# A macaron encoder block in split fp32: the norm's factor moved behind the SwiGLUs' last products, and the first bytes of its SBUF tiles moved

## The chip, the cores and the metric

The kernel runs on one core of a Trainium2 chip, in one launch. The metric is the device time of that launch in microseconds. The kernel before takes 2161.77 us, the median of three runs (2161.57 to 2161.9).

## What is computed

x is 1024 tokens by 1024 features in fp32; a SwiGLU has 2816 hidden features.

```python
def rmsnorm(x, g):
    return x * rsqrt(mean(x * x, -1) + eps) * g

def swiglu_ffn(x, w_in, w_out):
    gate, up = split(x @ w_in, 2)
    return (silu(gate) * up) @ w_out

h = x + 0.5 * swiglu_ffn(rmsnorm(x, norm_ffn1), ffn1_w_in, ffn1_w_out)
u = rmsnorm(h, norm_mix)
q, k, v, g_ret, p, gates = split(u @ w_in)
ret  = headwise_rmsnorm(retention(rotary(q), rotary(k) / 16, v)) * silu(g_ret)
pool = multiscale_pool(p)
gate = sigmoid(gates + gate_bias)
h = h + (gate[0] * (ret @ w_ret_up) + gate[1] * (pool @ w_pool_up)) @ w_out
h = h + 0.5 * swiglu_ffn(rmsnorm(h, norm_ffn2), ffn2_w_in, ffn2_w_out)
return rmsnorm(h, norm_final)
```

The factor of a norm, rsqrt(mean + eps), is one number for each token. It commutes with a matrix product, so the kernel multiplies un-normed features and applies the factor later. In `silu(gate) * up` the gate needs it before silu; the up half is only multiplied, so its factor may come at any later place, behind `w_out` too.

## The kernel before

**Products.** Activations lie with features on the 128 partitions and tokens along the free axis (two halves of 512). TensorE (PE) works on fp32 in two pieces: `split` (L153 to L155) makes a high part by a copy on ScalarE (ACT) and a low part by a subtraction on VectorE (DVE); `split_scaled` (L157 to L159) does so with a factor. `mm3` (L172 to L176) then makes each product from three matmuls, high x high (L174), high x low (L175), low x high (L176). The stationary operand is 128 x 128, "the weights" below; the moving operand is 128 x 512, or 128 x 256 at the second level.

**Strassen.** `strassen` (L421) forms a 2 x 2 block product from seven products on combinations of the weights' blocks (L11, S1 to S4, ...) and of the activations' blocks (R11, T1 to T4, ...), with results in PSUM banks `a`, `b` and `e`. Two of the seven, with R21 and with R22, are done for pairs of groups by another Strassen level (`common`, L527): three steps of 14 small products of three matmuls each. Their weights are the tiles `wx`, `ws12`, `ws34` and `wy`, and their moving operands are blocks `y1` to `y4` that `blocks` (L341) makes once for a norm, beside blocks of R21 and R22 themselves. This gives 43 blocks of 42 matmuls of 256 columns in the whole kernel: 15 in the first SwiGLU, 10 in the projections, 18 in the second SwiGLU.

**Order.** `Flow` (L57) runs over steps. Each step has a `prep` (loads, combinations and splits) and a `body` (matmuls and evacuation); a prep is issued LOOK = 4 steps ahead of its body. Everything else waits in one list of background work (`flow.add`), of which `rate` entries, one or two, are issued after each body. What stands under `soon()` gets a high priority. A scheduler orders each engine's instructions from this. All loads and stores go through SyncE's (SP's) queue.

**The SwiGLU's first half** (`ffn_in`, L699) has 22 groups, each one 128-row tile of gate and one of up. `evac` (L713) takes results out of PSUM. If the rows of the norm's factor (`nx.rb`, one 128 x 1024 tile with the factor of each token on all partitions) exist already, and the result is not to be added to another, the factor is multiplied in on the way (L718). Otherwise the plain value is written, and a multiplication by the factor goes into the background list (L722). Both are done for the gate and for the up half, by halves of 512 tokens. At a group's end (`end`, L724) come the silu (ACT, L728) and the product of gate and up in two halves (L731); for every second group the combinations of two hidden tiles that the next half needs are formed and stored to DRAM.

**The SwiGLU's second half** (`ffn_out`, L801) has the products p1, p6, p2, p7, p5, p3 and p4 (L819 on), each a loop over the 11 pairs of hidden tiles; p1 and p6 alternate, and so do p2 and p7. Eight tiles `acc` (128 features x 1024 tokens) are loaded with the residual at k = 6 of p1 (L829 to L832). `after1` to `after4` (L898 to L938) add each finished PSUM bank, times 0.5, to its quarters (`onto`, L891): P1 goes into a small tile `h` and from there into three quarters. Then `sink` takes a finished quarter on to the next norm (sums of squares). In the second SwiGLU the seventh product is turned round, with tokens on the partitions: `near` (L957) prepares the T4 blocks with a factor 0.5 and does two of four token tiles step by step, `far` the other two; `last.seed` and `last.finish` belong to the final norm (`Last`), which scales `dacc` and stores.

**Tiles.** All tiles come from pools whose buffers lie one behind another in SBUF. `weights` (L166) takes a tile of 1024 + LINE floats, LINE = 64, and lets the weights start `at` floats behind its beginning. `at` is 0 for first-level products. For the second level it is APART = 48 floats (192 bytes), except `wy` where the block `y4` lies in a buffer of the tag `t4`: those have 0 (`near`, L269 and L347, L547). `ss` tiles hold sums (8 floats). In the built program the first bytes within a partition are these:

| tile or tag | before | modulo 256 | after | modulo 256 |
|---|---|---|---|---|
| `ones_r` | 3040 | 224 | 3072 | 0 |
| `c2` (from) | 3552 | 224 | 3584 | 0 |
| `t4` (from) | 19936 | 224 | 19968 | 0 |
| `raw` (from) | 56800 | 224 | 56832 | 0 |
| `wt` (from; 4352 bytes each) | 73248 | 32 | 73472 | 0 |
| `mv` (from) | 95008 | 32 | 95232 | 0 |
| `tl` (from) | 209696 | 32 | 209920 | 0 |
| second-level weights inside `wt` | +192 | 224 | +88 | 88 |

The first byte of the weights less that of the moving operand, modulo 256, is as follows. First-level products have 0 before and after, since the tags `wt` and `mv` both lie at 32, later both at 0. Second-level products have 192 before where the block lies in `mv` or `tl`; where it lies in `t4`, `ws34` with `y3` has 0 and `wy` with `y4` has 64. After, all of them have 88. In the retention, the products with `kd` and those of the scores have 0, those with `sm` 192 and those of the state with `q` 64. After, all of these have 0.

Of the kernel before, what the change touches and what calls it, by code (L numbers as in the profile page):

```python
# [17 lines left out]
P = 128  # L18
S = 1024
# [71 lines left out]
def block_kernel(ctx: ExitStack, tc, x, x_tok, vecs, f1_in, f1_out, w_in, w_v, pool_w, w_ret, w_pool, w_o,  # L91
# [170 lines left out]
    class Next(Norm):  # L262


        def __init__(self, name, gain, keep=None):
            super().__init__(name)
            self.gain, self.keep = gain, keep
            self.M, self.Y, self.made, self.ready, self.tiles, self.t1s, self.rb = {}, {}, {}, set(), {}, {}, None
            self.near = set()  # L269

        def quarter(self, mt, tokens, tile):
            src = tile[:, tokens]
# [68 lines left out]
        def blocks(self, R, tags, over=False):  # L341

            left, x = dict(zip(("y3", "y2", "y4") if over else ("y1", "y3", "y2", "y4"), tags)), {}
            if left["y4"][0] == "t4":  # L347
                self.near.add(R)

            def sums(z):  # L350
                for i in range(2):
                    m = self.M[R, 2 * i + z]
                    v = c2(f"{self.name}x{i}{z}")
                    tt(v, m[:, 0].bitcast(F32), m[:, 1].bitcast(F32), ADD)
                    x.update({(i, j, z): half_of(v, j) for j in range(2)})

            def difference(n, z):

                x00, x01, x10, x11 = (x[i, j, z] for i in range(2) for j in range(2))
                to, p, q = {"y1": (x00, x01, x00), "y3": (x01, x11, x01), "y2": (x00, x11, x00),  # L360
                            "y4": (x00, x10, x00)}[n]
                tt(to, p, q, SUB)
                if n not in left:
                    m, at = self.M[R, z], HI
                else:
                    tag, bufs = left[n]
                    if (R, n) not in self.made:

                        self.made[R, n] = sb.tile([P, 2, H], F32R, tag=tag, bufs=bufs, name=f"{self.name}{R}{n}")
                    m, at = self.made[R, n], (LO, HI)[z]  # L370
                self.Y[R, n, z] = parts(m, at)
                split(m[:, 0, at], m[:, 1, at], to)
                if z and n == "y4":
                    self.ready.add(R)

            work = []
            for z in range(2):
                work.append(lambda z=z: (sums(z), difference("y1", z)))
                work.append(lambda z=z: difference("y3", z))
                work.append(lambda z=z: (difference("y2", z), difference("y4", z)))  # L380
            return work
# [145 lines left out]
    def common(nx, A, B, n):  # L527
# [171 lines left out]
    def ffn_in(nx, w, ops, name, start=None):  # L699
# [4 lines left out]
        def group(g):  # L704
            gate_up = {}

            def dest(which):
# [2 lines left out]
                    gate_up[tile] = (tl if start and g == 0 else t4)(f"{name}{'gu'[tile]}{g}")  # L710
                return half(gate_up[tile], j)

            def evac(which, in0, in1):  # L713
                j, dst = which[1], dest(which)
                if in1 is not None:
                    tt(dst, in0, in1, ADD)
                elif nx.rb is not None:
                    tt(dst, in0, half(nx.rb, j), MUL)  # L718
                    return
                else:  # L720
                    copy(dst, in0)
                flow.add(lambda: tt(dst, dst, half(nx.rms(), j), MUL))  # L722

            def end():  # L724
                gate, up = gate_up[0], gate_up[1]

                def swish():
                    act(gate, gate, AF.Silu)  # L728

                def times(j):  # L730
                    tt(half(up, j), half(gate, j), half(up, j), MUL)  # L731
# [66 lines left out]
    ops_done = {}  # L798


    def ffn_out(ops, ready, w, res, name, sink, end, last=None):  # L801

        R, T, B, T4 = ops
        t, acc = {}, {}
        S1, S2, S3 = {}, {}, {}

        def kept(store, n, k):
            if k % 2 == 0:  # L810
# [12 lines left out]
        def p1(k):  # L823
            flow.until(lambda: k in ready)
            r = tl(f"{name}r{k}")
            load(r, R[k])
            ra = raw(f"{name}ra{k}")
            load(ra, w[k, :, :S])
            if k == 6:  # L829
                for mt in range(KT):  # L830
                    acc[mt] = t4(f"{name}acc{mt}")
                    load(acc[mt], res[mt])  # L832
# [10 lines left out]
            return s2, half(t["r"], 1)  # L843

        def p2(k):
            r = tl(f"{name}q{k}")
# [8 lines left out]
        def p7(k):  # L855
            return half(S3[k // 2], k % 2), half(t["r"], 1)

        def p5(k):
            return half(S1[k // 2], k % 2), both("T1", k, lambda z: B[z][:, :H])

        def p3(k):
            return half(S2[k // 2], k % 2), both("R22", k, lambda z: T[z][:, H:])

        def p4(k):
            return both("L22", k, lambda z: w[z, :, 2 * H : 3 * H]), both("T4", k, lambda z: T4[z])

        bk = {}
# [20 lines left out]
        def quarter(mt, j):  # L888
            return half(acc[mt], j)

        def onto(mt, j, where, i, last=True):  # L891
            q = quarter(mt, j)
            with soon():
                stt(q, bk[where, i], 0.5, q, MUL, ADD)
            if last:
                flow.add(lambda: sink(mt, slice(j * H, (j + 1) * H), acc[mt]))

        def after1(i):  # L898
            h = c2(f"{name}p1{i}")
            with soon():  # L900
                act(h, bk["a", i], AF.Copy, scale=0.5)
                tt(quarter(i, 1), quarter(i, 1), h, ADD)

            def rest():
                for j in (1, 0):
                    tt(quarter(i + 4, j), quarter(i + 4, j), h, ADD)

            flow.add(rest)

        def after6(i):  # L910
            onto(i, 1, "b", i, False)

        def after2(i):
            onto(i, 0, "a", i)

        def after7(i):
            onto(i + 4, 1, "b", i, False)
            if last:

                onto(i + 4, 0, "b", i, False)  # L920
                if i == 3:
                    flow.add(*last.turned(acc))

        def after5(i):
            onto(i + 4, 1, "a", i)

        def after3(i):
            onto(i, 1, "a", i)
            if i == 3:
                end(0)  # L930

        def after4(i):
            onto(i + 4, 0, "b", i)
            if i == 3:
                end(1)

# [74 lines left out]
    x_sums = sb.tile([P, 8], F32, tag="ss", bufs=2, name="x_sums")  # L1011

    def x_square(t):
        r = tl(f"xs{t}")
# [15 lines left out]
    def ffn1():  # L1030
        for n, step in enumerate(ffn_in(first, f1_in, ops1, "a", lead)):
            flow.rate = 1 if n < 40 else 2
            yield step
        yield from ffn_out(ops1, ops_done["a"], f1_out, x, "b", mix.quarter, end1)

    mix = Next("n2", V_MIX, h1)

# [328 lines left out]
    class Unit:  # L1366
# [5 lines left out]
        def loads(self):  # L1372
# [9 lines left out]
            if self.nh == 0:  # L1382
                self.dec = sb.tile([P, H], F32, tag="dec", bufs=1, name=f"dec{self.h}")
                load(self.dec, decay[self.h])
                self.ss = sb.tile([P, 8], F32, tag="ss", bufs=2, name=f"ss{self.h}")
                self.O = {}

        def follow(self, u):
# [278 lines left out]
    class Last(Norm):  # L1667
# [15 lines left out]
        def turned(self, acc):  # L1683


            def gains():
                self.row = sb.tile([P, S], F32, tag="mv", bufs=N_MV, name=f"{self.name}row")
                load(self.row, g_row)
                self.ssq_e = sb.tile([P, 8], F32, tag="ss", bufs=2, name=f"{self.name}sse")

            def done(n):

# [72 lines left out]
    flow.run(chain(ffn1(), projections(), retention(), merge(), second(),  # L1765
                   ffn_out(ops2, ops_done.setdefault("c", set()), f2_out, h2, "d", fin.quarter, fin.end, fin)))
    flow.some(-1)


# [84 lines left out]
```

## Time and profile before

| | |
|---|---|
| median of three runs | 2161.77 us |
| the profiled execution | 2165.61 us |
| its span, first to last instruction | 2163.8 us |
| SwiGLU 1, first half | 0 to about 432 us |
| SwiGLU 1, second half | to about 667 us |
| projections | to about 1181 us |
| retention and pooling's products | to about 1370 us |
| merge and output projection | to about 1524 us |
| SwiGLU 2, first half | to about 1942 us |
| SwiGLU 2, second half and final norm | to 2164 us |

The stages are read from the names of the matmuls' outputs: a tile's name begins with the letter of its stage (`a` and `b` for the first SwiGLU's two halves, `c` and `d` for the second's), and digits are left out of the groups. The page gives the busy time of each engine with its share of the span, then slices, the chain of work that ended last, and groups of instructions. PE's matmuls are pipelined: one row of the timeline starts well before the one ahead of it has ended, so the time of a matmul is read from one start to the next and not from its own length. By the rows of stages, the retention keeps PE and DVE busy like this (columns: stretch, length, then for PE, weight load, DVE, ACT and POOL the busy time and count, the granted clock, the DMA engines' mean share and GB/s):

```profile
1181.00:1370.00 189.00, 188.19 (x1170) 167.93 (x1169) 150.77 (x300) 114.81 (x271) 0.00 (x0) 1.00 0.61 208
1942.00:2164.00 222.00, 215.11 (x967) 177.70 (x965) 165.85 (x292) 104.04 (x195) 0.00 (x0) 0.99 0.54 182
```

The second row is the last half of the second SwiGLU with the final norm, where PE is without work for 6.9 us, most of it behind the last matmul.

### The profile page before, as it was taken

What the parts mean: (1) busy time and instruction counts of PE and PEld (TensorE: products, weight loads), DVE (VectorE), ACT (ScalarE), POOL (GpSimd) and SP (SyncE); (2) the same over time, 40 slices, a digit from 0 to 9 for tenths busy, and PEclk for the clock granted to TensorE, in tenths of its full rate; (3) what the DMA queues carried; (4) which work ended last, traced back from release to release, by engine and by line L of the source; (5) the groups of instructions that cost most, each with busy time, mean ns of one, the idle gap of its engine ahead of it and who ended that gap; (6) DMA issues with size and microseconds to landing.
All of it is one profiled execution on the core that took longest, in us unless ns stands there. A gap on an engine that the chain in (4) does not pass through costs nothing.

```text
span 2163.8 us, 29697 instructions
## 1 busy us (share of the span) xinstructions
PE 2148.3 (99%) x10668; PEld 1816.2 (84%) x10668; DVE 1869.9 (86%) x3300; ACT 1088.1 (50%) x2047; POOL 0.2 (0%) x4
## 2 busy tenths in 40 slices
PE   9999999999999999999999999999999999999998
PEld 7888888888888888888888898888888888888887
DVE  8799899998778798899767877899999989999784
ACT  8544444545656444444426754446644444455463
POOL 0000000000000000000000000000000000000000
PEclk9999999999999999999999999999999999999999
DMA  7232323496323333333485567624132332359532
GB/s 255 75 118 99 115 93 124 159 337 211 127 93 98 117 127 108 115 110 116 154 268 192 166 227 255 220 92 161 64 120 100 106 104 93 117 183 336 177 122 78
DMA packets 117828, 320.92 MB, mean 148 GB/s; under 512 B 12976, under 2 KB 17200, under 8 KB 117680
## 3 DMA queue, kind: packets, MB, share of 16 engines
q1 hardware_dynamic: 117104, 317.97, 43.3%
q8 instruction: 83, 1.36, 0.3%
q10 hardware_dynamic: 576, 1.05, 0.1%
q14 instruction: 65, 0.53, 0.1%
HBM read 228.27 MB, written 90.70 MB: 147 GB/s over the span
## 4 chain that ended last, share of the span: by engine, by line
PE 89%; DVE 8%; DMA 1%; issue 1%; ACT 1%; SPq 0%; DVEq 0%; ACTq 0%
PE c_b L174 2%; PE c_b L176 2%; PE c_b L175 2%; PE c_e L176 2%; PE a_b L176 2%; PE a_b L174 2%; PE a_b L175 2%; PE c_e L175 2%; PE c_e L174 2%; PE a_e L176 1%; PE bp6b L176 1%; PE bp6b L175 1%; PE bp6b L174 1%; PE a_e L174 1%; PE a_e L175 1%; PE c_a L175 1%
## 5 line engine op out<-in xcount | busy, mean ns | idle before, releaser
L175 PE MATMUL c_b<-n3T,c_wS 128*128 128x512 f32 x176 | 68.5, 389 | 0.0
L176 PE MATMUL c_b<-n3T,c_wS 128*128 128x512 f32 x176 | 68.5, 389 | 0.0
L174 PE MATMUL c_b<-n3T,c_wS 128*128 128x512 f32 x176 | 68.3, 390 | 0.0
L174 PE MATMUL a_b<-n1T,a_wS 128*128 128x512 f32 x168 | 65.4, 389 | 0.0
L176 PE MATMUL a_b<-n1T,a_wS 128*128 128x512 f32 x168 | 65.4, 389 | 0.0
L175 PE MATMUL a_b<-n1T,a_wS 128*128 128x512 f32 x168 | 65.4, 389 | 0.0
L176 PE MATMUL a_a<-n1R,a_wL 128*128 128x512 f32 x120 | 47.0, 393 | 0.8 <-DVE a_wL L155 0.8
L175 PE MATMUL a_a<-n1R,a_wL 128*128 128x512 f32 x120 | 47.2, 393 | 0.0
L174 PE MATMUL a_a<-n1R,a_wL 128*128 128x512 f32 x120 | 47.1, 393 | 0.0
L175 PE MATMUL c_a<-n3R,c_wL 128*128 128x512 f32 x112 | 43.8, 391 | 0.0
L176 PE MATMUL c_a<-n3R,c_wL 128*128 128x512 f32 x112 | 43.7, 390 | 0.0
L174 PE MATMUL c_a<-n3R,c_wL 128*128 128x512 f32 x112 | 43.6, 389 | 0.0
L176 PEld LDWEIGHTS c_b<-n3T,c_wS 128*128 128x128 f32 x176 | 33.0, 188 | 6.9
L174 PEld LDWEIGHTS c_b<-n3T,c_wS 128*128 128x128 f32 x176 | 33.1, 188 | 6.8
L175 PEld LDWEIGHTS c_b<-n3T,c_wS 128*128 128x128 f32 x176 | 33.1, 188 | 6.8
L174 PEld LDWEIGHTS a_b<-n1T,a_wS 128*128 128x128 f32 x168 | 31.5, 188 | 6.7 <-ACT a_v L477 0.2
L175 PEld LDWEIGHTS a_b<-n1T,a_wS 128*128 128x128 f32 x168 | 31.5, 188 | 6.6
L176 PEld LDWEIGHTS a_b<-n1T,a_wS 128*128 128x128 f32 x168 | 31.5, 188 | 6.5
L176 PE MATMUL c_e<-n3T,c_wS 128*128 128x512 f32 x88 | 35.1, 399 | 0.5 <-DVE c_wS L155 0.4
L174 PE MATMUL c_e<-n3T,c_wS 128*128 128x512 f32 x88 | 34.4, 391 | 0.0
L176 PE MATMUL c_e<-n3T,c_wL 128*128 128x512 f32 x88 | 34.4, 391 | 0.0
L175 PE MATMUL c_e<-n3T,c_wL 128*128 128x512 f32 x88 | 34.4, 391 | 0.0
(3058 smaller groups left out, 8071.0 us busy)
## 6 DMA issues: line engine op xcount, KB each, us to landing
c_ra<-in_f_in SPq DMA_DIRECT2D x22, 512.0 KB, 3.6
c_rb<-in_f_in SPq DMA_DIRECT2D x22, 512.0 KB, 4.2
a_ra<-in_f_in SPq DMA_DIRECT2D x21, 512.0 KB, 3.6
a_rb<-in_f_in SPq DMA_DIRECT2D x21, 512.0 KB, 4.3
t<-au SPq DMA_DIRECT2D x11, 512.0 KB, 2.6
b<-ag SPq DMA_DIRECT2D x11, 512.0 KB, 2.7
r<-au SPq DMA_DIRECT2D x11, 512.0 KB, 3.6
br<-r SPq DMA_DIRECT2D x11, 512.0 KB, 6.1
```

Of the source, the lines that this page charges most:

```text
L174: mm(dst, w[0], m[0], start=start, stop=False, skip_group_check=True)
L175: mm(dst, w[0], m[1], start=False, stop=False, skip_group_check=True)
L176: mm(dst, w[1], m[0], start=False, stop=stop, skip_group_check=True)
```

## The change

It has two parts that do not depend on each other.

**The factor.** In `ffn_in` only the gate gets the factor, and where both halves of a gate are late, in one multiplication of 1024 columns; gate times up becomes one operation of 1024 columns as well. `ffn_out` is given the norm. At k = 6 of p1 it makes a tile with half the factor (`rows`, on ACT). `acc` is no longer loaded with the residual. Quarters are formed from the plain products (P1 kept in `p1s`, additions instead of a scaling with an addition), and a background entry `done` multiplies a finished quarter by half the factor, adds the residual and calls `sink`. `after2` multiplies straight out of PSUM. The residual comes in half tiles into `raw`, `c2` and `tl` buffers at k = 8 of p2, p7, p5, p3 and p4. In `near`, DVE multiplies each T4 block by half the factor first, and a plain `split` follows.

**The tiles' first bytes.** `ss` tiles take 128 bytes instead of 32 (`eights`), a tile of 32 bytes named `line` is put in front, and both shift all that comes behind, as in the table. APART becomes 22 floats (88 bytes), and the exception for `wy` goes.

PE's instructions stay the same in number, in almost the same order; the four sums `fin0sum` of the final norm come 25 matmuls later. DVE has 3180 instructions for 3300, ACT 2009 for 2003, SP 815 transfers for 799.

```diff
-LINE, APART = 64, 48
+LINE, APART = 64, 22
...
+    def eights(name):
+        return sb.tile([P, 32], F32, tag="ss", bufs=2, name=name)[:, :8]
...
+    cp.tile([P, 8], F32, name="line")
...
-            if left["y4"][0] == "t4":
-                self.near.add(R)
...
-            w["y"] = weights(b[src][:, HI], f"{A.name}wy{n}", 0 if R in nx.near else APART)
+            w["y"] = weights(b[src][:, HI], f"{A.name}wy{n}", APART)
...
+            later = []
             def evac(which, in0, in1):
-                j, dst = which[1], dest(which)
+                tile, j = which
+                dst, rms = dest(which), nx.rb
                 if in1 is not None:
                     tt(dst, in0, in1, ADD)
-                elif nx.rb is not None:
-                    tt(dst, in0, half(nx.rb, j), MUL)
+                elif not tile and rms is not None:
+                    tt(dst, in0, half(rms, j), MUL)
                     return
                 else:
                     copy(dst, in0)
-                flow.add(lambda: tt(dst, dst, half(nx.rms(), j), MUL))
+                if not tile:
+                    later.append(j)
...
-                def swish():
+                def scale():
+                    if len(later) == 2:
+                        tt(gate, gate, nx.rms(), MUL)
+                    else:
+                        for j in later:
+                            tt(half(gate, j), half(gate, j), half(nx.rms(), j), MUL)
                     act(gate, gate, AF.Silu)
-                def times(j):
-                    tt(half(up, j), half(gate, j), half(up, j), MUL)
-                flow.add(swish, lambda: times(0), lambda: times(1))
+                flow.add(scale, lambda: tt(up, gate, up, MUL))
...
+        def rows():
+            t["rb"] = sb.tile([P, S], F32, tag="mv", bufs=N_MV, name=f"{name}rb")
+            act(t["rb"], nx.rms(), AF.Copy, scale=0.5)
+        def residual(mts, j, tile, two=2):
+            for n in range(0, 4, two):
+                r = tile(f"{name}res{mts[n]}{j}")
+                for z, mt in enumerate(mts[n : n + two]):
+                    load(half(r, z), res[mt][:, j * H : (j + 1) * H])
+                    old[mt, j] = half(r, z)
...
-        def onto(mt, j, where, i, last=True):
+        def onto(mt, j, where, i, before=None):
             q = quarter(mt, j)
             with soon():
-                stt(q, bk[where, i], 0.5, q, MUL, ADD)
+                tt(q, bk[where, i], q if before is None else before, ADD)
+        def scale(q, src, j):
+            tt(q, src, half(t["rb"], j), MUL)
+        def done(mt, j, to=sink, scaled=False):
+            q = quarter(mt, j)
+            def end():
+                if not scaled:
+                    scale(q, q, j)
+                tt(q, q, old.pop((mt, j)), ADD)
+                if to:
+                    to(mt, slice(j * H, (j + 1) * H), acc[mt])
+            flow.add(end)
+        def after1(i):
+            p1s[i] = c2(f"{name}p1{i}")
+            with soon():
+                copy(p1s[i], bk["a", i])
+        def after2(i):
+            with soon():
+                scale(quarter(i, 0), bk["a", i], 0)
+            done(i, 0, scaled=True)
...
                 l, r = p4(k)
+                scale(r, r, 0)
                 L[k], X[k] = operand(l, f"{name}p4w{k}"), mv(f"{name}p4m{k}")
-                split_scaled(X[k][:, 0], X[k][:, 1], r, 0.5)
+                split(X[k][:, 0], X[k][:, 1], r)
```

More of the change, by code (lines that the diff above doesn't have):

```diff
@@ L798, in block_kernel, with ffn_out @@
     ops_done = {}
-    def ffn_out(ops, ready, w, res, name, sink, end, last=None):
+    def ffn_out(nx, ops, ready, w, res, name, sink, end, last=None):
         R, T, B, T4 = ops
-        t, acc = {}, {}
+        t, acc, old, p1s = {}, {}, {}, {}
         S1, S2, S3 = {}, {}, {}
+        def rows():
[7 more added lines that the diff above has]
+                    old[mt, j] = half(r, z)
+        TOP, LOW = range(4), range(4, 8)
         def kept(store, n, k):
@@ L829, in p1 @@
             if k == 6:
+                rows()
                 for mt in range(KT):
                     acc[mt] = t4(f"{name}acc{mt}")
-                    load(acc[mt], res[mt])
             t["x"] = half(ra, 0), half(ra, 1), both("L22a", k, lambda z: w[z, :, 2 * H : 3 * H])
@@ L845, in p2 @@
         def p2(k):
+            if k == FH - 3:
+                residual(TOP, 0, raw)
             r = tl(f"{name}q{k}")
@@ L855, in p7 @@
         def p7(k):
+            if last and k == FH - 3:
+                residual(LOW, 0, c2, 1)
             return half(S3[k // 2], k % 2), half(t["r"], 1)
         def p5(k):
+            if k == FH - 3:
+                residual(LOW, 1, raw)
             return half(S1[k // 2], k % 2), both("T1", k, lambda z: B[z][:, :H])
         def p3(k):
+            if k == FH - 3:
+                residual(TOP, 1, raw)
             return half(S2[k // 2], k % 2), both("R22", k, lambda z: T[z][:, H:])
         def p4(k):
+            if not last and k == FH - 3:
+                residual(LOW, 0, tl)
             return both("L22", k, lambda z: w[z, :, 2 * H : 3 * H]), both("T4", k, lambda z: T4[z])
@@ L933, in after4 @@
             onto(i + 4, 0, "b", i)
+            done(i + 4, 0)
             if i == 3:
@@ L1033, in ffn1 @@
             yield step
-        yield from ffn_out(ops1, ops_done["a"], f1_out, x, "b", mix.quarter, end1)
+        yield from ffn_out(first, ops1, ops_done["a"], f1_out, x, "b", mix.quarter, end1)
     mix = Next("n2", V_MIX, h1)
```

37 lines of the change are left out of this document (14 added, 23 removed).

## Prediction

> **What bounds the kernel now.** I read the page first: the shares by engine, the slices, then the chain that ended last.
>
> ```profile
> span 2163.8 us, 29697 instructions
> ...
> PE 2148.3 (99%) x10668; PEld 1816.2 (84%) x10668; DVE 1869.9 (86%) x3300; ACT 1088.1 (50%) x2047; POOL 0.2 (0%) x4
> ...
> DVE  8799899998778798899767877899999989999784
> ...
> PEclk9999999999999999999999999999999999999999
> ...
> PE 89%; DVE 8%; DMA 1%; issue 1%; ACT 1%; SPq 0%; DVEq 0%; ACTq 0%
> ```
>
> PE is busy for 99% of the span at full clock and has 89% of the chain. So the time is the sum of the matmuls' steps (start of one to start of the next) plus a few holes. An operation taken from DVE is worth only the hole that it made. The profiled execution took 2165.6 us, 3.8 us over the median of the three runs (2161.8); I work out differences against the former and take them off the latter.
>
> The steps stand in the timeline of PE. First the first-level products (512 columns), then the second-level ones (256), then two products of the retention (256).
>
> ```profile
> 1620.75 0.39 PE L176 MATMUL c_e<-n3T,c_wS 128*128 128x512 f32 x1
> ...
> 1626.87 0.39 PE L176 MATMUL c_b<-n3T,c_wS 128*128 128x512 f32 x1
> ...
> 1672.82 0.28 PE L174 MATMUL c_x<-n3R,c_wx 128*128 128x256 f32 x1
> ...
> 1677.78 0.39 PE L174 MATMUL c_a<-n3R,c_wL 128*128 128x512 f32 x1
> ...
> 1680.54 0.39 PE L174 MATMUL c_a<-n3R,c_wL 128*128 128x512 f32 x1
> ```
>
> ```profile
> 1183.26 0.28 PE L176 MATMUL st<-v,kd 128*128 128x256 f32 x1
> ...
> 1185.18 0.28 PE L174 MATMUL ob<-v,sm 128*128 128x256 f32 x1
> ...
> 1187.22 0.28 PE L174 MATMUL xb<-state,q 128*128 128x256 f32 x1
> ```
>
> From 1620.75 to 1626.87 lie 27 steps: 226.7 ns each. From 1672.82 to 1677.78 lie the 42 of a second-level block: 118.1. From 1183.26 to 1185.18 lie 16 of `kd`: 120.0. From there to 1187.22 lie 18 of `sm`: 113.3. Shape, types and clock of the last three are the same. What differs is where the weights lie against the moving operand. I call the distance of their first bytes, modulo 256, d. By the addresses listed ahead of this part, with the kernel, d is 0 for `kd`, 192 for `sm` and for most second-level products, 64 for `wy` with `y4`. So placement is worth up to 6.7 ns of a step, but d alone doesn't settle it: at d = 192 there are 113.3 and 118.1.
>
> **The change part by part.**
>
> *(a) Less DVE work ahead of the gates.* DVE loses the up half's factor and has one wide product for two narrow ones. The groups by shape and the wide form:
>
> ```profile
> L722 DVE TENSOR_TENSOR au<-au,n1rb 128x512 f32<-128x512 f32 x44 | 30.0, 685 | 0.0
> ...
> L731 DVE TENSOR_TENSOR au<-ag,au 128x512 f32<-128x512 f32 x44 | 29.4, 685 | 0.0
> ...
> L722 DVE TENSOR_TENSOR ag<-ag,n1rb 128x512 f32<-128x512 f32 x37 | 25.2, 684 | 0.1
> ```
>
> ```profile
> L1060 DVE TENSOR_TENSOR cos<-cos,n2rb x1: 1220/1220/1220, 754.4 to 754.4; 128x1024 f32<-128x1024 f32 x1
> ```
>
> ```profile
> 93.88 1.29 DVE L722 TENSOR_TENSOR au<-au,n1rb 128x512 f32<-128x512 f32 x2
> ```
>
> Narrow ones overlap at their ends: two take 1.29 us, so a step is 0.60 us; a wide one, 0.08 shorter than its 1.22, is 1.14. FFN1 has 44 + 44 + 37 narrow ones = 75 us; after the change 22 wide products, 15 wide and 7 narrow gate factors = 46 us. So 29 us less of DVE in FFN1, and likewise in FFN2. What PE gets of it is what it waits for. By stretches (PE, PEld, DVE, ACT, POOL busy, clock, DMA):
>
> ```profile
> 93.00:120.00 27.00, 27.00 (x129) 22.71 (x129) 27.00 (x48) 11.55 (x19) 0.00 (x0) 1.00 0.46 163
> 120.00:131.00 11.00, 9.97 (x42) 7.19 (x41) 10.53 (x26) 5.03 (x12) 0.00 (x0) 0.88 0.32 126
> 131.00:432.00 301.00, 299.11 (x1593) 257.12 (x1593) 279.69 (x507) 143.47 (x262) 0.00 (x0) 1.00 0.34 116
> 560.00:641.00 81.00, 81.00 (x359) 67.10 (x358) 58.37 (x94) 42.55 (x73) 0.00 (x0) 1.00 0.30 96
> 641.00:667.00 26.00, 26.00 (x122) 21.67 (x120) 23.55 (x38) 16.52 (x31) 0.00 (x0) 1.00 0.26 85
> 1524.00:1942.00 418.00, 416.15 (x2193) 356.90 (x2192) 391.31 (x720) 206.86 (x385) 0.00 (x0) 1.00 0.32 108
> 2059.00:2140.00 81.00, 80.88 (x376) 66.88 (x375) 61.13 (x109) 45.60 (x87) 0.00 (x0) 1.00 0.29 94
> ```
>
> ```profile
> 124.26 0.50 PE L174 MATMUL a_a<-n1R,a_wL 128*128 128x512 f32 x1
> ...
> 127.54 0.50 PE L176 MATMUL a_a<-n1R,a_wL 128*128 128x512 f32 x1 [0.77 <-DVE a_wL L155]
> ...
> 131.99 0.40 PE L174 MATMUL a_a<-n1R,a_wL 128*128 128x512 f32 x1
> ```
>
> Between 93 and 131 us DVE has no gap to speak of: the factors of the groups made before the rows of the norm existed fall due there beside the second-level sums. PE pays: 25 matmuls (9 wide, 16 narrow) between 124.26 and 131.99 take 7.73 us where 9 x 0.227 + 16 x 0.118 = 3.93 would do, and the granted clock falls to 0.88. Of DVE's groups in that stretch, these go or shrink:
>
> ```profile
> L722 DVE TENSOR_TENSOR au<-au,n1rb 128x512 f32<-128x512 f32 x8 | 5.3, 686 | 0.0
> ```
>
> Eight factors at a step of 0.60 are 4.8 us, more than the hole of 3.8. **-3.8.** In the rest of the two stages PE idles 301 - 299.11 = 1.9 and 418 - 416.15 = 1.9 us, in small waits for low halves of weights; DVE is busy 93% there and comes to about 86%. I take half: **-1.9** (bounds 0 and -3.8).
>
> *(b) More DVE work at the end of each FFN.* A quarter of the output now takes a factor and an addition: +12 DVE operations in FFN1's output stage (7.2 us), +27 in FFN2's (16.3 us), of which 11 are the factor on the T4 blocks. In FFN1 they fall between 560 and 667 us, where DVE idles 22.6 + 2.5 us. In FFN2 the first product's part loses 12 and the stretch from 2059 us gains 39 = 23.5 us, against 81 - 61.1 = 19.9 us free; the eight last scalings of `dacc` can slip behind the last product's preparation. The sums of squares slip with it, and PE's queue has them later: in the built program the four `fin0sum` stand 25 matmuls further back. I take **+0.5** (bounds 0 and 16.3). The residual's loads (16 half loads for 8 whole ones in each FFN, later in SP's queue) land three steps ahead, at 0.29 to 0.30 DMA share: nothing. The 35 us that DVE has less in all buy nothing else.
>
> *(c) Second-level products.* 43 blocks of 42 = 1806 matmuls, all at d = 88. No row shows 88. The ends are a transposition's step and `kd`:
>
> ```profile
> 1236.31 1.75 PE ot L1511 x16
> ```
>
> 1.75 / 16 = 109 ns is the shortest step with a new weight load that I find, 120.0 the longest settled one: 1806 times -8.7 and +1.9 ns, so -15.7 and +3.4 us. Between them stand two levels that the same distance shows, 118.1 and 113.3. Which one holds seems to depend on what ran before: `sm` comes out of the d = 0 run at once at 113, the second-level blocks come out of 512-column products and stay at 118. With one distance for all of a block, the lower level is as near as the upper one. I take 115.1, 3 ns off: **-5.4**.
>
> The Trainium skill ("TensorE: Matmul & The Clock Gate", "Step-by-step: what each phase is for") says that PE has two independent SBUF read ports and that "Loading the next tile's weights doesn't steal SBUF read bandwidth from the running matmul." By it this term would be 0, as in the first rival; the 120.0 and 113.3 speak against it.
>
> *(d) Retention.* All its tiles come to d = 0. The 144 `sm` products (18 in each of 8 units) go from 113.3 to 120: **+1.0**. Those with `q` may lose as much at most.
>
> *(e) First-level products after a block.* From 1677.78 to 1680.54 lie 12 steps of 230.0, 3.3 over the usual 226.7: 0.04 us a block, 33 blocks in the FFNs, 1.3 us, where the block ended at d = 0 or 64. I take **-0.8**. The other 512-column products, some 8000, keep d = 0 and I take them as unchanged; but all tiles move from 32 to 0 past 256, which no row shows.
>
> Sum: -3.8 - 1.9 + 0.5 - 5.4 + 1.0 - 0.8 = **-10.4**. The profiled execution would take 2155.2, the median **2151.4 us**.
>
> **The rivals.**
>
> *Placement does nothing.* Second-level steps stay at 118; terms (c) and (e) go: -4.2, **2157.6 us**. For it: the same d has both levels, so 88 may meet the upper one. Against: `kd` and `sm`.
>
> *88 is as bad as 0.* 120: (c) is +3.4, (e) goes, the whole is -0.8, **2161.0 us**. For it: no weights now start off a multiple of 32 bytes, and 88 is off it.
>
> *The end of FFN2 becomes DVE's.* Slower than before. From 2094 us on, DVE gains 27 operations, 16.3 us. A step of the last product takes 6 x 0.227 = 1.36 us of PE and now three DVE operations, 1.8 us, so it lives on the lead. If DVE has none, all 16.3 lie on the path: 2151.4 - 0.5 + 16.3 = **2167.2 us**. It passes the old time when over 10.9 of the 16.3 are uncovered. Against it: DVE idle times in this timeline show a lead,
>
> ```profile
> 2118.07 0.69 DVE L159 SCALAR_TENSOR_TENSOR dp4m<-dT,dp4m 128x512 fp32r<-128x512 f32 x1 [2.04 <-ACT dp4m L158]
> 2120.78 0.69 DVE L155 TENSOR_TENSOR dp4w<-dL,dp4w 128x512 fp32r<-128x512 f32 x1 [2.01 <-ACT dp4w L154]
> 2123.51 0.69 DVE L159 SCALAR_TENSOR_TENSOR dp4m<-dT,dp4m 128x512 fp32r<-128x512 f32 x1 [2.04 <-ACT dp4m L158]
> ```
>
> since it waits there for buffers that PE has not yet given back.
>
> *First-level products move too.* Each ns of their step is 8.0 us. If starting on 256 bytes takes off 1.5 ns of it, 2151.4 - 12 = **2139.4 us**; the 6.7 ns that placement is worth at 256 columns would be 54 us. The Trainium skill (same page, "Back-to-back issue gap") has 512 / 2.4 + 2.5, 216 ns, for a matmul of 512 columns; the row says 226.7, so there may be something to win, by that page an estimated 85 us. It may as well go the other way.
>
> **How the numbers follow.** Forecast (second-level steps clearly down, first-level ones as they are) 0.45; placement does nothing 0.20; as bad as 0: 0.13; DVE at the end 0.09; first-level products down 0.09, up 0.04. A change of 0.2%, 4.3 us, is about what a measurement of this kernel can tell from none: faster is below 2157.5, slower above 2166.1. The forecast and falling first-level steps are faster (0.54), the first rival lies at the border and goes half each way (0.10); the rest of it, the second rival and a part of the third are within it (0.25); slower 0.11. The range goes from 2139 (first-level steps down a little, or second-level ones near 109) to 2162, which takes in the first two rivals.
>
> **What would show it.** In the profile after: the steps of `c_x` and `c_y` at 113 to 116; no clock below 1 and no 0.77 us wait between 120 and 131 us; L722 gone from `au`; `sm` at 120; first-level steps at 226.7; PE without gaps from 2094 us on. It is wrong if first-level steps move by a nanosecond, or if PE waits for `dT` factors.

## The result, and the profile after

The changed kernel takes 2170.95 us (median of 5 runs, 2169.71 to 2171.46), the kernel before 2161.77 in the same session: 1.0042 of it, 95% interval 1.0027 to 1.0056, so 9.2 us slower where 10.4 faster was forecast. The profiled execution took 2170.95 us with a span of 2169.2.

First the page of the changed kernel, the lines that answer to those of before.

```profile
span 2169.2 us, 29623 instructions
...
PE 2144.7 (99%) x10668; PEld 1811.1 (83%) x10668; DVE 1839.2 (85%) x3180; ACT 1093.4 (50%) x2053; POOL 0.2 (0%) x4
...
PE 88%; DVE 8%; DMA 2%; issue 1%; ACT 1%; SPq 0%; ACTq 0%; DVEq 0%
```

DVE is busy 30.7 us less (1869.9 before) and PE 3.6 us less (2148.3), yet the span is 5.4 longer: what was added is PE's waiting. Where it stands, the same stretches show (columns as in the table of stretches above):

```profile
120.00:131.00 11.00, 11.00 (x56) 9.12 (x56) 10.65 (x22) 7.06 (x13) 0.00 (x0) 1.00 0.14 46
131.00:432.00 301.00, 296.55 (x1585) 254.11 (x1584) 255.59 (x440) 139.25 (x256) 0.00 (x0) 1.00 0.34 118
560.00:641.00 81.00, 81.00 (x359) 67.07 (x358) 66.14 (x107) 39.27 (x66) 0.00 (x0) 1.00 0.44 138
641.00:667.00 26.00, 26.00 (x124) 21.65 (x123) 25.04 (x42) 17.01 (x31) 0.00 (x0) 1.00 0.17 61
667.00:1181.00 514.00, 508.29 (x2458) 428.60 (x2456) 432.20 (x735) 228.90 (x421) 0.00 (x0) 0.99 0.42 142
1524.00:1942.00 418.00, 414.22 (x2193) 354.84 (x2192) 365.89 (x645) 207.59 (x386) 0.00 (x0) 1.00 0.31 107
2059.00:2140.00 81.00, 81.00 (x374) 66.82 (x373) 76.71 (x130) 43.74 (x81) 0.00 (x0) 1.00 0.37 114
```

The hole from 120 to 131 us is gone, and the last half of the second SwiGLU has none. But in the first halves of both SwiGLUs PE now idles 4.5 and 3.8 us (1.9 and 1.9 before), although DVE is busy 24 and 25 us less there; and behind 667 us it idles 5.7 where there was nothing. By PE's first matmul of each stage (the projections' first product starts at 641.6 us before, not at about 667 as the table of stages ahead has it):

| stage | before | after | difference |
|---|---|---|---|
| start to first product | 6.2 | 6.1 | -0.1 |
| SwiGLU 1, first half | 426.0 | 423.5 | -2.5 |
| SwiGLU 1, second half | 209.4 | 209.6 | +0.1 |
| projections to retention | 727.9 | 735.4 | +7.5 |
| merge | 154.4 | 154.4 | 0 |
| SwiGLU 2, first half | 418.1 | 418.1 | -0.1 |
| SwiGLU 2, second half and the end | 221.8 | 222.1 | +0.3 |

**The seam behind the first SwiGLU.** PE's timeline of the changed kernel, and two stretches of it:

```profile
682.79 0.39 PE L180 MATMUL p0a<-n2R,p0wL 128*128 128x512 f32 x1
688.89 0.79 PE L178 MATMUL p0e<-n2T,p0wS 128*128 128x512 f32 x1 [5.71 <-ACT p0wS L158]
689.48 0.63 PE L179 MATMUL p0e<-n2T,p0wS 128*128 128x512 f32 x1
689.91 0.63 PE L180 MATMUL p0e<-n2T,p0wS 128*128 128x512 f32 x1
```

```profile
688.80:692.00 3.20, 3.11 (x7) 2.36 (x8) 3.20 (x7) 3.20 (x8) 0.00 (x0) 0.50 0.42 169
692.00:700.00 8.00, 8.00 (x36) 6.59 (x35) 7.97 (x18) 4.21 (x9) 0.00 (x0) 0.99 0.56 183
```

One step takes 6.10 us in place of 0.23, and the granted clock is then 0.50 for 3.2 us (0.43 us a step), 1.6 us more: 7.5 together, all of the third row. The releaser named is ACT; what made ACT late is mainly DVE's queue. First the changed kernel, then the kernel before:

```profile
672.46 0.15 DVE L214 TENSOR_SCALAR n2v<-n2sum 128x8 f32<-128x8 f32 x1
...
684.29 0.68 DVE L1133 TENSOR_TENSOR t0A<-t0A,n2rb 128x512 f32<-128x512 f32 x1
...
685.83 0.68 DVE L437 TENSOR_TENSOR p0S<-p0rb 128x512 f32<-128x512 f32 x1
...
686.76 0.68 DVE L450 TENSOR_TENSOR p0rb<-p0ra,p0rb 128x512 f32<-128x512 f32 x1
```

```profile
667.94 0.17 DVE L209 TENSOR_SCALAR n2v<-n2sum 128x8 f32<-128x8 f32 x1 [2.43 <-PE n2sum L223]
...
671.47 0.69 DVE L155 TENSOR_TENSOR p0wL<-p0ra,p0wL 128x512 fp32r<-128x512 f32 x1 [1.74 <-ACT p0wL L154]
...
679.59 0.69 DVE L435 TENSOR_TENSOR p0S<-p0rb 128x512 f32<-128x512 f32 x1
...
681.72 0.69 DVE L448 TENSOR_TENSOR p0rb<-p0ra,p0rb 128x512 f32<-128x512 f32 x1
```

The mixing norm's sum is read 4.5 us later, after the 25.0 of 26 us that DVE worked up to 667 us. The two idle times of before, 2.43 and 1.74 us, were most of the lead: from 665.5 to 684.4 us, where `p0wS` is split, DVE idles 5.1 us there. After them the factors of t0 and t1 (`n2rb`) stand in DVE's queue without a gap ahead of p0's weights, and `p0rb`, from which `p0wS` is split, comes 5.0 us later.

**The gate stages.** The groups of PE that wait now, from the page of the changed kernel (the last column is idle time before them and what ended most of it):

```profile
L180 PE MATMUL c_b<-n3T,c_wS 128*128 128x512 f32 x176 | 69.3, 394 | 2.4 <-DVE c_wS L159 2.3
L178 PE MATMUL c_b<-n3T,c_wS 128*128 128x512 f32 x176 | 68.3, 390 | 1.4 <-ACT c_wS L158 1.4
...
L180 PE MATMUL a_b<-n1T,a_wS 128*128 128x512 f32 x168 | 65.9, 392 | 2.0 <-DVE a_wS L159 2.0
L178 PE MATMUL a_b<-n1T,a_wS 128*128 128x512 f32 x168 | 65.5, 390 | 1.4 <-ACT a_wS L158 1.4
```

Before, all of them had 0.0. They wait for the weights S2. DVE's timeline in the second SwiGLU, the changed kernel first:

```profile
1693.48 0.68 DVE L757 TENSOR_TENSOR cu<-cu,cg 128x512 f32<-128x512 f32 x1
...
1694.68 0.68 DVE L762 TENSOR_TENSOR cm<-cu,cu 128x512 f32<-128x512 f32 x1
1695.28 0.68 DVE L437 TENSOR_TENSOR c_S<-c_S,c_ra 128x512 f32<-128x512 f32 x1
```

```profile
1685.86 0.68 DVE L435 TENSOR_TENSOR c_S<-c_S,c_ra 128x512 f32<-128x512 f32 x1
...
1689.15 0.68 DVE L744 TENSOR_TENSOR cg<-cu 128x512 f32<-128x512 f32 x1
```

L757 and L762 (`w2`, `w3`) combine hidden tiles for the second half, which needs them far later. Before, S2 of the next group (L435) came ahead of the first of these operations (`w1`, L744); now it comes behind the last. From 1685 us to the end of the stage this is so in all seven rounds of the two traces.

**The first bytes.** A second-level block of 42 steps, and 18 steps with `sm`, in the changed kernel:

```profile
1726.98 0.28 PE L178 MATMUL c_x<-n3R,c_wx 128*128 128x256 f32 x1
...
1731.76 0.40 PE L178 MATMUL c_e<-n3T,c_wS 128*128 128x512 f32 x1
```

```profile
1188.88 0.28 PE L178 MATMUL ob<-v,sm 128*128 128x256 f32 x1
...
1191.04 0.28 PE L178 MATMUL xb<-state,q 128*128 128x256 f32 x1
```

4.78 / 42 = 113.8 ns and 2.16 / 18 = 120.0 ns. Over all second-level steps below 140 ns the mean goes from 117.8 to 114.3; steps of 512 columns below 250 ns stay at 227.03.

### The profile page after: what moved, and what is told of

Read it like the earlier page. It is cut to its first block, busy times and chain, and to the rows that moved or that the text cites. A ratio compares the mean times of both kernels' runs of the same rounds, so it can differ in the third digit from the quotient of the medians.

```text
span 2169.2 us, 29623 instructions
## 1 busy us (share of the span) xinstructions
PE 2144.7 (99%) x10668; PEld 1811.1 (83%) x10668; DVE 1839.2 (85%) x3180; ACT 1093.4 (50%) x2053; POOL 0.2 (0%) x4
## 4 chain that ended last, share of the span: by engine, by line
PE 88%; DVE 8%; DMA 2%; issue 1%; ACT 1%; SPq 0%; ACTq 0%; DVEq 0%
PE c_b L180 2%; PE a_b L180 2%; PE c_b L179 2%; PE a_b L178 2%; PE c_b L178 2%; PE a_b L179 2%; PE a_e L178 1%; PE a_e L180 1%; PE a_e L179 1%; PE bp6b L179 1%; PE bp6b L178 1%; PE bp6b L180 1%; PE a_a L179 1%; PE a_a L178 1%; PE a_a L180 1%
## 5 line engine op out<-in xcount | busy, mean ns | idle before, releaser
L158 ACT CAST a_wS<-a_S 128x512 fp32r<-128x512 f32 x45 | 27.1, 621 | 17.1 <-DVE a_S L437 9.6
L178 PE MATMUL c_e<-n3T,c_wS 128*128 128x512 f32 x88 | 34.4, 391 | 0.0
```

Of the source, the lines that this page charges most:

```text
L158: copy(hi, src)
L178: mm(dst, w[0], m[0], start=start, stop=False, skip_group_check=True)
```

## Experiments

Theory A: the seam's wait comes from the operations that the change puts on DVE at the first SwiGLU's end. Theory B: the short waits in the gate stages come from the background list, which has fewer entries and so runs ahead. Against both stands that the first bytes cost time. The medians of before were 2163.1 to 2163.4 us in these sessions; ratios are to those.

**e1, the first bytes alone** (before with `line`, `eights`, APART 22 and no `near`).

> The kernel before with the tiles' first bytes of the changed one (bases on 256 bytes, second-level weights at byte 88, no exception for wy), the factor where it was. Theory (the loss is all in the factor's move; the new first bytes are a gain): the second-level steps go from 117.8 to about 114.2 ns as in the changed kernel, 1806 x 3.6 = 6.5 us less, sm and the products with q lose 1.5, so about 2156.5 us, and no wait at p0wS. Rival (the new first bytes cost time somewhere that the steps of PE don't show, as in later DMAs or slower DVE operations): 2162 us or more.

Measured: 2160.64 us, 0.9987 (0.9978 to 0.9997). The steps came as expected (second level 114.3 ns, sm 120.0), and p0e waits for nothing. Yet 2.7 us came of the 5 expected. Set against e3, which differs in where the second-level weights start alone, the trace says where the rest is: at their mean steps the second-level products save 6.2 us, and steps that wait (over 140 or 250 ns) lose 2.7 us more. I read this as PE reaching the next weights sooner and waiting for them.

**e2, the factor alone** (changed kernel, tiles as before).

> The changed kernel with all tiles where they lay before (APART 48, the exception for wy, no line, small ss tiles): only the factor moves. Theory: the loss of the changed kernel, 9.2 us by the medians, without the 5 to 6.5 us that the first bytes give back, so 2176 to 2178 us, with a wait of 5 us or more at p0wS. Rival (the first bytes are the cause): 2165 us or less.

Measured: 2172.36 us, 1.0042 (1.0027 to 1.0057), with 5.69 us before p0e. The factor is all of the loss. That the first bytes bring nothing on top of it was not expected (2176 to 2178 us had been); stretches of e2 show the larger part of why:

```profile
131.00:428.00 297.00, 294.51 (x1572) 253.27 (x1571) 253.64 (x439) 138.49 (x255) 0.00 (x0) 1.00 0.34 119
1535.00:1940.00 405.00, 402.02 (x2114) 344.64 (x2114) 351.30 (x620) 198.41 (x370) 0.00 (x0) 1.00 0.31 107
```

PE idles 2.5 and 3.0 us here; in the changed kernel, with faster second-level steps, it idles 4.5 and 3.8 in the same two stretches. Of some 5 us that the steps save, waiting steps take back 4.2 over the whole trace.

**e3, the bases alone** (before with `line` and `eights`).

> The kernel before with the tiles' bases on 256 bytes only: APART stays 48 and wy keeps its exception. If a base on 256 bytes is worth nothing by itself, only sm, q and wy with y4 move, to 120 ns: +1.0, +0.5 and 114 x 2 ns, so 2163 to 2164 us. If 88 is not what matters and the bases are, the second-level steps fall to about 114 ns here too: 2156 to 2157 us.

Measured: 2163.03 us, 1.0001 (0.9991 to 1.001). Second-level steps at 192 stay at 117.5 to 117.8 ns, sm goes to 120.0. A base on 256 bytes is worth nothing; the 88 is. `wy` with a `y4` in `t4` comes to 0 here and was expected at 120 ns; it has 118.4.

**e4, the factor in the second SwiGLU only.** The first one's `evac`, `end` and `ffn_out` (here `ffn_out_old`) are those of before.

```diff
...
-        yield from ffn_out(first, ops1, ops_done["a"], f1_out, x, "b", mix.quarter, end1)
+        yield from ffn_out_old(ops1, ops_done["a"], f1_out, x, "b", mix.quarter, end1)
```

> The changed kernel with the first SwiGLU as before (factor on gate and up, residual in acc from the start, narrow products); the second keeps the move, and the first bytes stay. Theory A (the seam: 12 more DVE operations at the first SwiGLU's end make the mixing norm late, PE waits 5.9 us for p0wS and runs 1.6 us at a lower clock behind it): that wait goes, so do 8 us of short waits for c_wS's like in the first SwiGLU, and the wait of 4 us at 123 to 131 us comes back, 2159 to 2163 us. Rival B (the projections' wait comes from elsewhere, the loss is in the order of the gate's work): the wait at p0wS stays and the time is over 2166 us.

Measured: 2164.01 us, 1.0003 (0.9994 to 1.0012), 8.4 us below the changed kernel's ratio, p0e without a wait: theory A, 1 us above the expected 2159 to 2163 us. The waits for c_wS in the second SwiGLU remain.

**e5, the entries put back.**

```diff
+            def rest():
+                pass
...
                 if not tile:
                     later.append(j)
+                if in1 is not None or rms is None:
+                    flow.add(rest)
...
-                flow.add(scale, lambda: tt(up, gate, up, MUL))
+                flow.add(scale, lambda: tt(up, gate, up, MUL), rest)
```

> The changed kernel with empty entries in the background list wherever the change took an entry out (the up half's factors, the second half of gate times up), so that as many entries are drained for each step as before. DVE's operations stay those of the changed kernel. Theory B (the short waits of PE for c_wS in both SwiGLUs, 8.3 + 5.9 us in the changed kernel, come from the shorter list: the combinations for the hidden tiles come earlier and stand in DVE's queue ahead of the weights' S2, which in the built program now comes behind them and here comes ahead of them again): these waits fall to 6 us or less in all, and the time is 6 to 9 us below the changed kernel, 1.000 to 1.002 of the kernel before. Rival (the wide operations of 1.14 us hold DVE's queue, whatever the order): the waits stay, ratio 1.004. Theory A: the wait at p0wS is untouched by this.

Measured: 2163.39 us, 1.0002 (0.9992 to 1.0011). Stretches of e5, then of the changed kernel, then p0e and DVE's queue in e5:

```profile
131.00:428.00 297.00, 296.60 (x1587) 255.09 (x1586) 257.59 (x444) 140.84 (x258) 0.00 (x0) 1.00 0.35 121
1535.00:1935.00 400.00, 399.71 (x2130) 343.28 (x2129) 351.49 (x621) 197.89 (x368) 0.00 (x0) 1.00 0.31 109
```

```profile
131.00:428.00 297.00, 292.55 (x1567) 250.81 (x1566) 251.59 (x435) 138.18 (x255) 0.00 (x0) 1.00 0.34 116
1535.00:1935.00 400.00, 396.22 (x2094) 339.08 (x2093) 349.14 (x616) 197.78 (x368) 0.00 (x0) 1.00 0.31 106
```

```profile
684.02 0.79 PE L178 MATMUL p0e<-n2T,p0wS 128*128 128x512 f32 x1 [5.71 <-ACT p0wS L158]
```

```profile
1722.29 0.68 DVE L437 TENSOR_TENSOR c_S<-c_S,c_ra 128x512 f32<-128x512 f32 x1
1722.89 0.68 DVE L758 TENSOR_TENSOR cg<-cu 128x512 f32<-128x512 f32 x1
```

S2 (L437) stands ahead of `w1` (L758) again. With the same DVE operations in another order PE idles 0.4 and 0.3 us instead of 4.5 and 3.8, 7.5 us less, and the time falls by 8.6 us by the two ratios. So theory B holds and the wide operations are not at fault. The seam's wait is the same to 0.01 us: the two causes are independent.

**e6, less at the very end of the first SwiGLU.**

In the first SwiGLU `after7` puts the factor on P1 and adds the residual, which is loaded in p7 and no longer in p4; `after4` is left with two operations for three.

```diff
...
-                copy(quarter(i + 4, 0), p1s[i])
+                q = quarter(i + 4, 0)
+                scale(q, p1s[i], 0)
+                flow.add(lambda: tt(q, q, old.pop((i + 4, 0)), ADD))
...
-            onto(i + 4, 0, "b", i)
-            done(i + 4, 0)
+            q = quarter(i + 4, 0)
+            with soon():
+                scale(bk["b", i], bk["b", i], 0)
+                tt(q, bk["b", i], q, ADD)
...
```

> The changed kernel, but in the first SwiGLU the last quarters (tokens 0 to 511 of features 512 to 1023) take the factor on P1 and the residual behind p7, and at the end of p4 only the bank's factor and one addition are left: 2 operations for a quarter at the very end instead of 3, 8 instead of 12 for the four. Theory A (the seam is DVE's, each operation there costs its step): PE's wait at p0wS falls by about 4 x 0.6 = 2.4 us or a little more with the clock, ratio about 1.003. Rival (the wait comes from the residual's late loads in p4): these loads are gone from p4, so the wait falls by more than 4 us, ratio 1.002 or less.

**e7, more at the very end, on the kernel of e1.** Between p4's addition and the next norm `after4` gets two idle operations for each of four quarters.

```diff
...
+                for _ in range(2):
+                    tt(q, q, q, ALU.max)
...
```

> The kernel of e1 (factor as before, new first bytes) with two idle DVE operations (the maximum of a quarter with itself, values unchanged) for each of the four last quarters of the first SwiGLU, between p4's addition and the next norm: 8 x 0.60 = 4.8 us of DVE just where the change adds its last eight. Theory A1 (DVE has no lead left at the end of the first SwiGLU, the last operations go through to PE one to one): PE waits 4 us or more for p0wS, 5 us over e1. Theory A2 (the wait needs all of the 24 operations that the change adds from p5 on): less than 2 us over e1.

Measured: e6 2169.54 us, 1.0028 (1.0016 to 1.004); e7 2162.65 us, 0.9997 (0.9988 to 1.0007). p0e in e6 and in e7:

```profile
687.97 0.80 PE L178 MATMUL p0e<-n2T,p0wS 128*128 128x512 f32 x1 [3.88 <-ACT p0wS L158]
```

```profile
685.80 0.50 PE L177 MATMUL p0e<-n2T,p0wS 128*128 128x512 f32 x1 [1.24 <-ACT p0wS L157]
```

Four operations less, 2.4 us of DVE, take 1.83 us off the wait, and the ratio is the 1.003 expected; the late residual isn't the wait's cause, since without its loads in p4 the wait falls by less than the 4 us of that rival. Eight more, 4.8 us, on a kernel without the wait make one of 1.24 and a median 2.0 us over e1's. Neither A1 (4 us or more) nor A2 (less than 2 us over e1) is quite right: there is a lead of some 3.5 us, of the size of the idle times of 2.43 and 1.74 us before, and beyond it operations at the seam go for the most part through to PE.

**e8, e11, e12: other distances, first-level weights too** (the kernel of e1 with `weights(src, name, at=APART)` as the default; APART 22, 32 and 16).

> The kernel of e1 with the weights of the first-level products at byte 88 as well (all weights of 512-column products but the turned ones). If the distance between weights and moving operand costs a 512-column product what it costs one of 256 columns, its step falls by up to 6 ns: 7900 x 6 = 47 us, 2113 us. If a step of 512 columns is set by its columns alone, nothing moves: 227.0 ns and the time of e1.

> The kernel of e8 with 128 bytes for 88, for first- and second-level weights. By the steps seen so far (512 columns: 227.0 at 0, 233.1 at 88; 256 columns: 120 at 0, 113 to 118 elsewhere) 512 columns lose here too, 230 to 233 ns, and the second level lies between 113 and 118. If 88 is bad for 512 columns only because it is no multiple of 32 or 64, their step is 227 here.

> The same with 64 bytes. Expected as for 128 bytes; the three distances together tell whether the step of 512 columns falls or rises with the distance, or only has 0 as its best point.

Measured: 2204.39 us (1.0188, interval 1.0173 to 1.0204), 2206.33 and 2203.66 us (the last two one run each). Steps of 512 columns at 88 bytes (35 of them) and at 64 (24):

```profile
1639.67 0.39 PE L178 MATMUL c_a<-n3R,c_wL 128*128 128x512 f32 x1
...
1647.84 0.39 PE L177 MATMUL c_b<-n3T,c_wS 128*128 128x512 f32 x1
```

```profile
1644.30 0.39 PE L177 MATMUL c_e<-n3T,c_wS 128*128 128x512 f32 x1
...
1649.90 0.39 PE L177 MATMUL c_e<-n3T,c_wS 128*128 128x512 f32 x1
```

233.4 and 233.3 ns, and 232.7 in the mean at 128, against 227.0 at 0: some 8000 steps by 6 ns are 48 us, of which e8 shows 44 against e1; steps that wait lose 4 us less. A second-level block at 128 and two at 64 bytes, by e11 and e12:

```profile
1624.28 0.28 PE L177 MATMUL c_x<-n3R,c_wx 128*128 128x256 f32 x1
...
1629.26 0.40 PE L177 MATMUL c_e<-n3T,c_wL 128*128 128x512 f32 x1
```

```profile
1622.74 0.28 PE L177 MATMUL c_x<-n3R,c_wx 128*128 128x256 f32 x1
...
1627.51 0.39 PE L177 MATMUL c_e<-n3T,c_wL 128*128 128x512 f32 x1
```

```profile
159.36 0.28 PE L177 MATMUL a_x<-n1R,a_wx 128*128 128x256 f32 x1
...
164.31 0.39 PE L177 MATMUL a_e<-n1T,a_wL 128*128 128x512 f32 x1
```

The first gives 118.6 ns, the second 113.6, the third, at 64 bytes as well, 117.9; the means over all second-level steps without a wait are 118.7 at 128 and 115.4 at 64. The mean at 64 mixes two levels: blocks without a wait stand at 113.5 in the projections and mostly at 117.8 in the first SwiGLU. So 256 columns do best at 88 among the distances tried, 512 columns at 0, and the distance alone doesn't set the step. The hope of a gain from the first level has no support; the expectation for e8, as far as it hoped for one, was wrong in sign.

**e9 and e10, versions with what was learned.** Both move all `t4` tiles 192 bytes further, so that sm and q stand as before. e10 is e1 with that; e9 is e4 with that and with e5's entries.

> The first SwiGLU as before; the second with the factor moved and the empty entries of e5; the new first bytes, but all t4 tiles 192 bytes further, so that sm and q stand to their moving operands as before the change (192 and 64) and y3 and y4 in t4 come to 152. If the ledger holds, this is e4 (ratio 1.0003) less about 4 us of waits for c_wS in the second SwiGLU and less 1.5 us in the retention: 0.9975 to 0.9985 of the kernel before, no wait at p0wS. Rival (what the second SwiGLU's gate stage saves comes back as other waits): 0.999 or more.

> The kernel of e1 with all t4 tiles 192 bytes further. sm goes back from 120.0 to 113.4 ns and q from 119.9 to 116.4: 1.5 us less than e1, ratio 0.998. If what decides is not the distance but the base of the tile, sm stays at 120. The 228 products with y3 and y4 at 152 show whether a distance other than 88 has 113 or 118 ns.

Measured: e10 2159.78 us, 0.9984 (0.9975 to 0.9993); e9 2159.13 us, 0.9979 (0.997 to 0.9988). sm is back at 113.4 ns and q at 116.5 (116.4 in e9); wy at 152 bytes has 118.0. e9 beats both kernels, by 4.3 us the one before. But it is 0.7 us from e10, less than either's interval: the factor's move in the second SwiGLU, with the entries put back, is worth nothing that these runs can tell. For the first SwiGLU this is not settled. By PE's first matmuls its first half takes 418.3 us in e5 and 422.3 to 423.9 in the four runs with the new first bytes and that SwiGLU as before (e1, e4, e9, e10); the projections take 735.6 us in e5 and 726.8 to 727.6 in those four. So in these single traces the move gains some 4 us in the one and loses some 8 in the other, and no run has the gain without the loss.

## Why the prediction was wrong

The frame held: PE's steps and holes make the time, and an operation taken from DVE is worth only its hole. It was applied to the places where operations leave, and not where they arrive.

- **(a), first half, -3.8: right in mechanism.** The hole at 120 to 131 us is gone and the clock stays at 1.00; in e4, where the first SwiGLU is as before, PE idles 1.0 us there again and the clock falls to 0.84. No run measures its size apart from the rest of the stage.
- **(a), second half, -1.9: wrong in sign.** "DVE is busy 93% there and comes to about 86%. I take half": the busy share fell as said (255.6 of 301 is 85%), but the idle time rose by 2.6 and 1.9 us. The share says nothing about who stands ahead of whom. The change also takes entries out of the list that paces the background work, which the prediction did not count as an effect at all. e5 shows it: with the entries put back PE idles 0.4 and 0.3 us there. For the two first halves together (a), (c) and (e) ask for -10.6 us, 33 of the 43 blocks counted; e5's trace has 11.0 less than before, (c) with more of it than forecast and (e) with none.
- **(b), +0.5: the step that failed.** "In FFN1 they fall between 560 and 667 us, where DVE idles 22.6 + 2.5 us": idle time ahead of an operation is no room for it. In the changed kernel DVE still idles 14.9 us between 560 and 641 us, and PE waits all the same. What p4 releases, from 641.6 us on, has little but the idle time behind it, 2.43 + 1.74 us, and then a queue without a gap. It costs 7.5 us with the clock: within the term's bounds of 0 and 16.3, but far from the 0.5 in the sum. The count was low as well: the quarters take 52 operations for 36, so +16 and not +12, and from p5 on 36 for 12. In the second SwiGLU, where I looked for the danger, PE waits for none of the 27.
- **(c), -5.4: right, and a little small.** 117.8 to 114.3 ns over 1806 steps is -6.3. That is in part luck: no row showed 88, the 115.1 was a choice between two levels, and at 128, just as untried, the runs show 118.7. And only part of it reaches the time: 2.7 us in e1 with the 1.5 lost in the retention, and nothing measurable on top of the factor (e2), since waits for DVE take it back. The Trainium skill ("TensorE: Matmul & The Clock Gate", "Step-by-step: what each phase is for") says that loading the next weights takes no SBUF read bandwidth from the running matmul. The prediction read from it that this term would be 0, and held two rows against it. No run here measures that bandwidth; e1 and e8 measure that placement moves the step, in both directions.
- **(d), +1.0: right** for sm (113.4 to 120.0 ns), and the products with q lose another 0.5.
- **(e), -0.8: wrong.** The first twelve steps of 512 columns after a block have 228.8 ns in the mean before and 229.0 after: those behind blocks with R22 fall from 230.4 to 228.8, those behind blocks with R21 rise from 227.5 to as much.
- **The rivals.** The slower one had the mechanism, a stage's end that becomes DVE's, at the wrong SwiGLU. I dismissed it for a lead that DVE has in the second SwiGLU and never asked for the lead at the first one's end.

Put in their measured sizes (the hole with its forecast 3.8) the terms come to -3.8 + 4.5 + 7.5 - 6.3 + 1.5 + 0 = +3.4 us against 5.4 in the spans. Most of the rest lies in the two first halves. I take it for short waits that PE's busy time covers; this isn't shown, and the first SwiGLU's first half alone differs by 1.6 us among traces with the same program there (e1, e4, e9, e10).

## What to carry to other kernels

Before moving work off a busy engine, look at the place where it lands: count the operations there, and hold them against the idle time that comes after their release and before the next consumer, not against the busy share of the stage. Where background work is paced by entries, fewer or wider entries reorder the queue even if they only remove work; keep the pacing when you merge them. A gain in steps of the bounding engine is worth its full size only while its feeder has lead; of e1's 6.2 us of second-level steps, 1.5 of them lost in the retention, 2.7 reached the time.

## What the runs showed of the hardware

Where weights begin against the moving operand, modulo 256 bytes, moves the step of these fp32 matmuls in both directions. With 512 columns it is 227.0 ns at 0 and 232.7 to 233.1 at 64, 88 and 128. With 256 columns in the second-level blocks it is 119.4 at 0 (`ws34` with `y3` before; `wy` with `y4` in e3 has 118.4), 115.4 at 64, 114.3 at 88, 118.7 at 128, 118.0 at 152 and 117.8 at 192 (means of steps without a wait). The distance isn't all: sm runs at 113.4 with 192, and at 64 the same kind of block stands at 113.5 in the projections and at 117.8 in the first SwiGLU. What makes it so stays open.

A wait of 5.71 us cost 1.6 us more by a granted clock of 0.50 in the 3.2 us after it. The Trainium skill ("TensorE: Matmul & The Clock Gate", "What's actually happening") has the clock halved after an idle window of about 3.4 us and restored after as long a busy one. The waits at the seam agree: after 3.88 us in e6 the clock is 0.50 from 688.0 to 690.8 us, and after 1.24 us in e7 it stays at 1.00. The hole of the kernel before does not fit that rule by itself: from 124 to 128 us PE idles 1.03 us in all, 0.77 at most at once, and the clock is still 0.50 from 129 to 131 us.
